# A transformer block in seven-product matmuls: first three column pairs interleaved at the start of mixer and FFN, one weight load moved, part of a norm moved to ScalarE

## The chip, the cores and the metric

One core of a Trainium2 chip runs the whole kernel. TensorE (PE) multiplies, VectorE (DVE), ScalarE (ACT) and GpSimd (POOL) work on tiles of 128 partitions, and SyncE (SP) issues most of the DMAs. The metric is device time in microseconds (us) of one execution; the median of three is 1564.4 us (1561.85 to 1564.85).

## The reference, cut to what matters

```
a = RMSNorm(x; norm_pre_mix)                       # x: 1024 tokens x 1024
q, k, v, r, low, u, sv, g1, g2 = split(a @ w_in)   # 1024 x 7184
y_gla = GLA(q, k, v, low; 4 heads, 64-token chunks) * silu(r) @ w_branch_gla
y_sgu = gelu(u) * spatial_mix(LayerNorm(gelu(sv))) @ w_branch_sgu
m  = sigmoid(g1) * y_gla + sigmoid(g2) * y_sgu
x1 = x  + RMSNorm(m @ w_out; norm_post_mix)
h  = RMSNorm(x1; norm_pre_ffn)
out = x1 + RMSNorm((silu(h @ w_a) * (h @ w_b)) @ w_ffn_out; norm_post_ffn)   # d_ff 2816
```

All of it is float32. GLA carries a state per head along 16 chunks of 64 tokens.

## The kernel before

**Products.** Each large matmul is done by the Strassen-Winograd scheme: seven half-size products instead of eight, with sums and differences of the quarters of both operands, and of the results. A product takes 12 matmuls of 128x512: four slices of the contraction, and for each slice three terms, because every operand is split into a high part (`hi`, a copy that ACT rounds to fp32r, L86) and a low part (`lo`, the rest, which DVE subtracts, L87). The three terms hi x hi, hi x lo, lo x hi are L110, L111 and L112 of `prod3`. So a product waits for an ACT instruction and then for a DVE instruction on both of its operands.

**Streams.** A `Pair` is two columns of 128 of a weight matrix: su, kq, v, r, sv, g1 and g2 are pairs of w_in (28 of them), f0 to f21 are pairs of w_ffn_in (22). `Pair.prepare(m)` makes product m's weight operand on DVE and ACT, `Pair.product(m)` runs its 12 matmuls, `collect` adds the result up. `Stream.todo` lists products in the order in which PE takes them; weights are prepared two ahead (`LEAD`). A lone pair goes 1, 7, 6, 5, 2, 4, 3. Only the first two pairs of a stream go in step, as 1, 2, 5, 7, 6, 4, 3 of both in turn, since at the start of a stream its left operand comes in piece by piece: products 1 and 2 need only tokens 512 to 1023 (`Operands.first`), product 5 needs the sum of two quarters of tokens 0 to 511 (`second`), product 4 one of them (`fourth`), and products 7, 6 and 3 need differences (`rest`).

**Stages.** x is loaded, normed, transposed on PE (tp_a) and split (the operand `a`; names ah5, al5 are hi and lo of product 5). The mixer stream runs 28 pairs; after its 14 first products the low-rank gate and then, as a background task stepped between products, the chunk states of GLA: u (update, PE), st (state, DVE, L599), o (readout, PE), on (ACT), ot (transpose). Two branch products follow, `bs` (ys) and `bl` (yg, seven products of 48 matmuls); yg's results are gated in `gla_final` by g1t and mt, loaded by SP into slots of the pool px (11 slots of 512 KB), and split into mh and ml. w_out multiplies mh, ml in four passes (token half and column half: 1,0; 1,1; 0,1; 0,0), each with eight weights w_wo, four of them in px. After the last two passes a token tile gets its two norms: `rs_pm` and `rs_pf` are inverse roots (a 128x1 power on POOL), xr is the residual (DVE, L1058), mix its normed copy (DVE, L1062). `Hs.tile` transposes it (tp_h on PE, copies hraw on ACT) and the FFN stream begins.

**Order.** The tile framework's scheduler puts the instructions of the recorded program on each engine's queue; on a queue they run in order. A `tc.manual_schedule` keeps the recorded order for the engines it names, `tc.issue_after` puts an instruction behind another.

## Time and profile before

| | |
|---|---|
| median of three runs | 1564.4 us |
| profiled execution | 1566.38 us, span 1564.5 us (1.9 us lie around the span) |
| mean granted TensorE clock | 0.992 of 2.4 GHz |
| PE busy | 1531.6 us, 98% of the span |
| DVE busy | 1134.8 us, 73% |
| ACT busy | 655.1 us, 42% |
| POOL busy | 178.7 us, 11% |

PE's busy time counts a matmul from issue to its end, and successive matmuls overlap, so 98% doesn't mean that only 2% could be saved: at half the clock PE is as busy as at full clock and does half as much.

### The profile page before, as it was taken

How to read it: one execution, taken by the hardware profiler on the slowest of the kernel's cores; microseconds unless marked ns; L12 is line 12 of the kernel's file. 1: busy time of each engine (PE TensorE's matmuls, PEld its weight loads, DVE VectorE, ACT ScalarE, POOL GpSimd, SP SyncE). 2: the span in 40 equal slices, each digit the busy share in tenths (PEclk: the TensorE clock that was granted, in tenths of full speed). 3: DMA queues.
4: the chain of work that ended last, by engine and by line, in shares of the span. 5: the costliest groups of instructions: out<-in, count | busy, mean ns of one | idle time of the engine just before them, and what ended most of it. 6: DMA issues, size and time to landing. Idle time of an engine off the chain costs nothing.

```text
span 1564.5 us, 19759 instructions
## 1 busy us (share of the span) xinstructions
PE 1531.6 (98%) x7061; PEld 1249.5 (80%) x7061; DVE 1134.8 (73%) x1854; ACT 655.1 (42%) x1074; POOL 178.7 (11%) x274
## 2 busy tenths in 40 slices
PE   7999999999999999999999989999999999999998
PEld 5778777687888888888877868888888888888886
DVE  7956676577978878657686689777777777565547
ACT  8475334244344343533443663333333333363442
POOL 2211111102211111000000120111111100000002
PEclk9999999999999999999999999999999999999999
DMA  4433344245654464588972633565555543775653
GB/s 163 126 95 96 120 151 166 76 148 167 238 195 155 145 212 141 177 317 305 332 239 81 204 120 101 187 204 176 197 184 185 176 133 101 284 273 173 226 161 128
DMA packets 181812, 276.06 MB, mean 176 GB/s; under 512 B 10777, under 2 KB 108593, under 8 KB 181714
## 3 DMA queue, kind: packets, MB, share of 16 engines
q1 hardware_dynamic: 157714, 190.35, 38.0%
q0 software_dynamic: 24000, 84.44, 14.7%
q8 instruction: 56, 0.92, 0.2%
q14 instruction: 42, 0.34, 0.1%
HBM read 188.47 MB, written 86.28 MB: 176 GB/s over the span
## 4 chain that ended last, share of the span: by engine, by line
PE 91%; DVE 6%; issue 1%; ACT 1%; DMA 1%; POOL 0%; DVEq 0%; SPq 0%; POOLq 0%; ACTq 0%
PE f_m L110 9%; PE f_m L111 9%; PE f_m L112 9%; PE fo L110 4%; PE fo L112 4%; PE fo L111 4%; PE g_m L110 3%; PE g_m L111 3%; PE g_m L112 3%; PE wo L112 2%; PE wo L111 2%; PE wo L110 2%; PE kq_m L112 2%; PE kq_m L111 2%; PE v_m L112 2%; PE v_m L111 2%
## 5 line engine op out<-in xcount | busy, mean ns | idle before, releaser
L110 PE MATMUL f_m<-hh,w_f 128*128 128x512 f32 x616 | 240.7, 391 | 5.2 <-ACT hh L86 5.2
L111 PE MATMUL f_m<-hl,w_f 128*128 128x512 f32 x616 | 240.4, 390 | 0.0
L112 PE MATMUL f_m<-hh,w_f 128*128 128x512 f32 x616 | 240.2, 391 | 0.0
L110 PEld LDWEIGHTS f_m<-hh,w_f 128*128 128x128 f32 x616 | 116.1, 189 | 29.9 <-ACT hh L86 5.8
L111 PEld LDWEIGHTS f_m<-hl,w_f 128*128 128x128 f32 x616 | 116.2, 189 | 24.2
L112 PEld LDWEIGHTS f_m<-hh,w_f 128*128 128x128 f32 x616 | 116.1, 188 | 24.2
L111 PE MATMUL fo<-fow,foa 128*128 128x512 f32 (+1 forms) x315 | 120.9, 384 | 0.0
L112 PE MATMUL fo<-fow,foa 128*128 128x512 f32 (+1 forms) x315 | 120.9, 384 | 0.0
L110 PE MATMUL fo<-fow,foa 128*128 128x512 f32 (+1 forms) x315 | 118.9, 385 | 0.5 <-DVE foc L914 0.5
L87 DVE TENSOR_TENSOR w_f<-wsum_f,w_f 128x512 fp32r<-128x512 f32 x88 | 60.5, 688 | 51.2 <-ACT w_f L86 50.7
L86 ACT ACTIVATE w_f<-wsum_f 128x512 fp32r<-128x512 f32 x88 | 55.3, 629 | 99.2 <-PE f_m L112 59.3
L111 PE MATMUL g_m<-al,w_g 128*128 128x512 f32 x224 | 88.3, 394 | 0.0
L110 PE MATMUL g_m<-ah,w_g 128*128 128x512 f32 x224 | 88.1, 393 | 0.0
L112 PE MATMUL g_m<-ah,w_g 128*128 128x512 f32 x224 | 87.8, 392 | 0.0
L86 ACT ACTIVATE w_f<-raw_f 128x512 fp32r<-128x512 f32 x66 | 41.4, 630 | 101.6 <-PE f_m L112 93.1
L87 DVE TENSOR_TENSOR foa<-fora,foa 128x1024 fp32r<-128x1024 f32 (+1 forms) x42 | 47.6, 1133 | 42.7 <-ACT foa L86 42.6
L86 ACT ACTIVATE foa<-fora 128x1024 fp32r<-128x1024 f32 (+1 forms) x42 | 41.5, 988 | 73.4 <-DMA fora<-fs_d 58.0
L110 PEld LDWEIGHTS fo<-fow,foa 128*128 128x128 f32 x315 | 59.2, 188 | 12.4 <-DVE foc L914 0.7
L111 PEld LDWEIGHTS fo<-fow,foa 128*128 128x128 f32 x315 | 59.2, 188 | 11.8
L112 PEld LDWEIGHTS fo<-fow,foa 128*128 128x128 f32 x315 | 59.2, 188 | 11.7
L87 DVE TENSOR_TENSOR fow<-forw,fow 128x1024 fp32r<-128x1024 f32 (+1 forms) x42 | 47.5, 1130 | 9.9 <-ACT fow L86 9.6
L112 PE MATMUL wo<-w_wo,ml 128*128 128x512 f32 x128 | 50.2, 396 | 2.6 <-DVE ml L87 2.6
(379 smaller groups left out, 3694.2 us busy)
## 6 DMA issues: line engine op xcount, KB each, us to landing
raw_f<-in_w_ffn_in SPq DMA_DIRECT2D x88, 256.0 KB, 3.3
fora<-fs_d SPq DMA_DIRECT2D x35, 512.0 KB, 4.5
w2e<-in_w_ffn_out SPq DMA_DIRECT2D x44, 256.0 KB, 4.3
fs_d<-f_o POOLq DMA_DIRECT2D x22, 512.0 KB, 3.8
ws_d<-w2e POOLq DMA_DIRECT2D x22, 512.0 KB, 3.8
forw<-ws_d SPq DMA_DIRECT2D x20, 512.0 KB, 4.6
raw_g<-in_w_in SPq DMA_DIRECT2D x16, 512.0 KB, 3.7
g_d<-g_o POOLq DMA_DIRECT2D x16, 512.0 KB, 4.2
```

Source lines behind the costliest of these rows:

```text
L86: a = nc.scalar.activation(hi, src, AF.Copy)
L87: return a, nc.vector.tensor_tensor(out=lo, in0=src, in1=hi, op=ALU.subtract)
L110: nc.tensor.matmul(acc, lhsT=lh, rhs=rh, start=first, stop=False, skip_group_check=onto)
L111: nc.tensor.matmul(acc, lhsT=lh, rhs=rl, start=False, stop=False, skip_group_check=onto)
L112: nc.tensor.matmul(acc, lhsT=ll, rhs=rh, start=False, stop=last, skip_group_check=onto)
```

## The change

It has five parts. (1) Both streams begin with three pairs: products 1 and 2 of the first two in turn, then 1 and 2 of the third, then 5, 7, 6, 4 and 3 of all three in turn. The third pair's raw weights live in the pool `pl`, its products take a buffer from both PSUM pools. For these pairs the weight differences are made in place, and product 5's result is copied straight into its half of the output tile. In the mixer the three pairs are fetched ahead, and the low-rank sums come after six products, where they came after four. (2) `fourth` is done just ahead of `rest`'s last part. (3) The weights of w_out's first pass are loaded and split between the two branches, where they were loaded during the second. (4) The second norm of token tiles 0, 1 and 2 is a scaled copy on ACT in place of DVE's three-operand instruction; its gain is applied when the transposed tile is copied, which takes eight 128x128 copies in place of two 128x512. Tile 3 stays as it was. (5) As the FFN begins, PE keeps the recorded order for its first 21 products, some weights are prepared behind named instructions, and the first silu (with its table load) is put behind the hi part of product 7's operand; until then the result is copied plainly.

```diff
-        def tile(self, row, tt):
+        def tile(self, row, tt, gains=None):
             r = 1 - tt // 4
             cols = slice((tt % 4) * P, (tt % 4) * P + P)
             for c in range(2):
                 b = tbank(f"tp_{self.name}{tt}{c}")
                 for j in range(4):
                     nc.tensor.transpose(b[:, j * P : (j + 1) * P], row[:, (c * 4 + j) * P : (c * 4 + j + 1) * P], ident)
-                nc.scalar.activation(self.quad(r, c)[:, :, cols], by4(b), AF.Copy)
+                if gains is None:
+                    nc.scalar.activation(self.quad(r, c)[:, :, cols], by4(b), AF.Copy)
+                    continue
+                for j in range(4):
+                    nc.scalar.activation(self.quad(r, c)[:, j, cols], b[:, j * P : (j + 1) * P], AF.Copy,
+                                         scale=gains[:, c * 4 + j : c * 4 + j + 1])
...
+                if m == 3:
+                    for i in range(2):
+                        nc.vector.tensor_tensor(out=s4[i], in0=a12[:, two[i]], in1=s1[:, two[i]], op=ALU.subtract)
+                    for tt in range(4):
+                        self.fourth(tt)
...
-                    self.last = split(hi[:, two[i]], lo[:, two[i]], src)[1]
+                    ins = split(hi[:, two[i]], lo[:, two[i]], src)
+                    self.last = ins[1]
+                    if m == 7:
+                        self.hi7 = ins[0]
...
+            self.trio = False
+            self.pool = (pr, "raw")
...
-                t = pr.tile([P, 4, 256], F32, tag="raw", name=f"raw_{self.name}{k}")
+                t = self.pool[0].tile([P, 4, 256], F32, tag=self.pool[1], name=f"raw_{self.name}{k}")
...
+                src = w12 if self.trio and m == 7 else py.tile([P, 4, P], F32, tag="Y", name=f"wsum_{self.name}{m}")
...
+            new = tbank if self.trio and m == 6 else bank
...
-                    self.p5 = [slot(f"{self.name}_p5", (P, 512))]
+                    self.out[1] = slot(f"{self.name}_o1")
+                    self.p5 = [self.out[1][:, 512:1024]]
...
+        def __init__(self, pairs, A):
             self.A = A
-            self.todo = []
-            self.hold = 11 if twin else 0
-            if twin:
-                a, b = pairs[:2]
-                self.todo += [(p, m) for m in (1, 2, 5, 7, 6, 4, 3) for p in (a, b)]
-                pairs = pairs[2:]
-            for p in pairs:
+            self.hold = 17
+            trio = pairs[:3]
+            for p in trio:
+                p.trio = True
+            trio[2].pool = (pl, "L")
+            self.todo = [(p, m) for part in (trio[:2], trio[2:]) for m in (1, 2) for p in part]
+            self.todo += [(p, m) for m in (5, 7, 6, 4, 3) for p in trio]
+            for p in pairs[3:]:
                 self.todo += [(p, m) for m in ORDER]
...
-                p.prepare(m)
+                with tc.issue_after(behind[self.ready].ins) if self.ready in behind else ExitStack():
+                    p.prepare(m)
...
-        wa = pl.tile([P, KT, 32], F32, tag="L", name="wa")
+        wa = slot("wa", (P, KT, 32))
...
     low_rank_weights()
-    stream.run(4)
+    stream.fetch(3)
+    stream.run(6)
     low_rank_sums()
-    for tt in (0, 1, 2, 3):
-        A.fourth(tt)
-    stream.run(2)
+    stream.run(3)
     A.rest()
-    stream.run(8)
+    stream.run(11)
     heads[0]["decays"] = bg.add(decays(*low_rank()))
-    stream.run(28, 2)
+    stream.run(22, 2)
...
-    bs.run()
-    bl.run()
...
+    wo = I["w_out"][0]
+
+    def out_weights(half, j):
+        return wide_weights(wo, list(range(KT)), j, f"wo{half}{j}", lambda k: (pw, "w") if k < 4 else (px, "X"))
+
+    bs.run()
+    wo10 = out_weights(1, 0)
+    bl.run()
...
+    first_silu = []
...
             if half == 1 and self.first:
-                with tc.issue_after(Hs.after[0].ins):
-                    nc.scalar.activation(o, src, func[0])
+                nc.scalar.activation(o, src, AF.Copy)
+
+                def silu():
+                    with tc.issue_after(Hs.hi7.ins):
+                        nc.scalar.activation(o, o, func[0])
+
+                first_silu.append(silu)
...
-        p.first = i % NK == 0
+        p.first = i % NK == 0 or i == 1
...
-        w = wide_weights(wo, list(range(KT)), j, f"wo{half}{j}", lambda k: (pw, "w") if k < 4 else (px, "X"))
+        w = wo10 if (half, j) == (1, 0) else out_weights(half, j)
...
-                xt = load(f"xr_{tt}", x[tt * P : (tt + 1) * P, :])
+                if tt in (2, 3):
+                    xt = slot(f"xr_{tt}")
+                    nc.sync.dma_start(out=xt, in_=x[tt * P : (tt + 1) * P, :])
+                else:
+                    xt = load(f"xr_{tt}", x[tt * P : (tt + 1) * P, :])
...
                 rs = rsqrt_mean(ss[:, 3:4], D, f"pf{tt}")
-                nc.vector.scalar_tensor_tensor(out=mix, in0=xt, scalar=rs, in1=g_pf, op0=ALU.mult, op1=ALU.mult)
-
-                def after(mix=mix, tt=tt):
-                    Hs.tile(mix, tt)
+                light = tt in (0, 1, 2)
+                if light:
+                    nc.scalar.activation(mix, xt, AF.Copy, scale=rs)
+                else:
+                    last = nc.vector.scalar_tensor_tensor(out=mix, in0=xt, scalar=rs, in1=g_pf, op0=ALU.mult,
+                                                          op1=ALU.mult)
+
+                def after(mix=mix, tt=tt, light=light):
+                    Hs.tile(mix, tt, g_pfT if light else None)
...
-    fstream.run(4)
-    fstream.prepare(6)
-    for tt in (0, 1, 2, 3):
-        Hs.fourth(tt)
-    Hs.rest()
-    fstream.run(8)
+    fstream.fetch(3)
+    fstream.prepare(4)
+    lo5 = Hs.after[1]
+    behind.update({4: last, 5: last, 6: last, 7: last, 8: lo5, 9: lo5, 10: lo5, 11: lo5})
+    with tc.manual_schedule(engines={mybir.EngineType.PE}):
+        fstream.run(9)
+        with tc.issue_after(lo5.ins):
+            Hs.rest()
+        behind.clear()
+        for f in first_silu:
+            f()
+        fstream.run(12)
```

Three places show how the queues move.

PE, in the middle of the mixer, before: the last two matmuls of v3's product 6 (v3 is the fourth v pair), the transposes wspT of the spatial weights, and GLA's readout o_23 with what follows it (u, st, o, on, ot as above; the digits are head and step).

```order
L112 MATMUL v3_m6_2670<-ah6_527,w_v36_2590 128x512
L581 MATMUL u_261_2645<-v_21_2358,kk_2_2289 128x256 x2
L691 MATMUL wspT_2660<-ident_106,wsp_2528 128x128 x4
L608 MATMUL o_23_2712<-st_233_2688,kq2_o1_1793 64x256
L608 MATMUL o_23_2712<-st_232_2687,kq2_o1_1793 64x256
L608 MATMUL o_23_2712<-st_231_2686,kq2_o1_1793 64x256
L608 MATMUL o_23_2712<-st_230_2685,kq2_o1_1793 64x256
L696 MATMUL rowsum_2717<-wT_2659,allone_2531 128x512
L635 MATMUL ot_230_2762<-ident_106,on_22_2650 128x128 x2
L635 MATMUL ot_231_2768<-ident_106,on_22_2650 128x128 x2
```

The same place in the change; ahead of these rows stand v3's product 6, readout o_20, updates u_22, wspT and the rest of o_21.

```order
L630 MATMUL o_21_2642<-st_210_2615,kq2_o1_1729 64x256
L603 MATMUL u_240_2647<-v_21_2482,kk_2_2418 128x256
L603 MATMUL u_241_2648<-v_21_2482,kk_2_2418 128x256
L603 MATMUL u_240_2647<-v_21_2482,kk_2_2418 128x256
L603 MATMUL u_241_2648<-v_21_2482,kk_2_2418 128x256
L718 MATMUL rowsum_2653<-wT_2589,allone_2458 128x512
L657 MATMUL ot_210_2698<-ident_106,on_20_2580 128x128 x4
L657 MATMUL ot_211_2704<-ident_106,on_20_2580 128x128 x4
L630 MATMUL o_22_2765<-st_223_2737,kq2_o1_1729 64x256
L630 MATMUL o_22_2765<-st_222_2736,kq2_o1_1729 64x256
```

Before, one state step stood between product 6 and product 5 of v3; now three (o_20, o_21, o_22) stand there, with no product between them.

DVE, as yg ends, before: ygc are the sums of yg's results, gated by g1t and mt, ml01 the lo part that w_out's first pass needs.

```order
L873 TENSOR_TENSOR ygc10_6687<-yg_72_6451,ygc01_6264 128x512
L87 TENSOR_TENSOR w_wo104_6827<-raw_wo104_6825,w_wo104_6827 128x512
L873 TENSOR_TENSOR ygc10_6687<-yg_73_6452,ygc01_6264 128x512
L957 TENSOR_TENSOR ygc10_6687<-ygc10_6687,g1t100_6691 128x512 x2
L957 TENSOR_TENSOR ygc10_6687<-ygc10_6687,g1t102_6711 128x512 x2
L958 TENSOR_TENSOR ygc10_6687<-ygc10_6687,mt100_6694 128x512 x2
L873 TENSOR_TENSOR ygc01_6264<-yg_50_6526,ygc01_6264 128x512
L958 TENSOR_TENSOR ygc10_6687<-ygc10_6687,mt102_6714 128x512
L87 TENSOR_TENSOR w_wo105_6830<-raw_wo104_6825,w_wo105_6830 128x512
L958 TENSOR_TENSOR ygc10_6687<-ygc10_6687,mt102_6714 128x512
L873 TENSOR_TENSOR ygc01_6264<-yg_51_6527,ygc01_6264 128x512
L87 TENSOR_TENSOR w_wo106_6835<-raw_wo106_6833,w_wo106_6835 128x512
```

The same place in the change.

```order
L894 TENSOR_TENSOR ygc10_6718<-yg_70_6480,ygc01_6295 128x512
L87 TENSOR_TENSOR ml11_6622<-ygc11_6543,mh11_6621 128x512
L894 TENSOR_TENSOR ygc10_6718<-yg_71_6481,ygc01_6295 128x512
L894 TENSOR_TENSOR ygc10_6718<-yg_72_6482,ygc01_6295 128x512
L894 TENSOR_TENSOR ygc10_6718<-yg_73_6483,ygc01_6295 128x512
L978 TENSOR_TENSOR ygc10_6718<-ygc10_6718,g1t100_6722 128x512 x2
L978 TENSOR_TENSOR ygc10_6718<-ygc10_6718,g1t102_6742 128x512 x2
L979 TENSOR_TENSOR ygc10_6718<-ygc10_6718,mt100_6725 128x512 x2
L979 TENSOR_TENSOR ygc10_6718<-ygc10_6718,mt102_6745 128x512 x2
L87 TENSOR_TENSOR ml01_6721<-ygc10_6718,mh01_6720 128x512
L894 TENSOR_TENSOR ygc01_6295<-yg_50_6557,ygc01_6295 128x512
```

The splits of w_wo are gone from this stretch (all eight of them stand between rows of ys now), and the ml01 splits follow the gating of ygc10 at once.

ACT, as the FFN begins, before: hh5, hh4 and hh7 are the hi parts of the left operand for products 5, 4 and 7, f0_o0 and f11_o0 the outputs to which the silu is applied.

```order
L86 ACTIVATE hh5_7522<-hraw20_7520 128x4x128
L86 ACTIVATE hh4_7732<-hraw11_7518 128x4x128
L86 ACTIVATE hh5_7522<-hraw20_7520 128x4x128
L1025 ACT_TABLE_LOAD
L1025 ACTIVATE f0_o0_7711<-f0_m1_7661 128x512
L1025 ACTIVATE f11_o0_7730<-f11_m1_7679 128x512
L86 ACTIVATE hh7_7744<-hraw10_7511 128x1024 x2
L86 ACTIVATE hh6_7752<-hraw20_7520 128x1024 x2
```

The same place in the change.

```order
L86 ACTIVATE w_f15_7794<-wsum_f15_7792 128x512
L1052 ACTIVATE f1_o0_7790<-f1_m1_7758 128x512
L86 ACTIVATE w_f07_7813<-raw_f00_7605 128x512
L86 ACTIVATE hh7_7852<-hraw10_7510 128x1024 x2
L1056 ACT_TABLE_LOAD
L1056 ACTIVATE f0_o0_7734<-f0_o0_7734 128x512
L1056 ACTIVATE f11_o0_7751<-f11_o0_7751 128x512
L1056 ACTIVATE f1_o0_7790<-f1_o0_7790 128x512
L318 ACTIVATE f0_o1_7810<-f0_m5_7797 128x512
L86 ACTIVATE w_f117_7832<-raw_f110_7614 128x512
```

The table load and the silus stood ahead of hh7; now they stand behind it, but w_f15, w_f07 and three plain copies of outputs (two of them some rows earlier) stand ahead.

## Rows read from the trace of the kernel before

**Rows 1.** The page, busy time, share of the span and instructions of each engine.

```profile
PE 1531.6 (98%) x7061; PEld 1249.5 (80%) x7061; DVE 1134.8 (73%) x1854; ACT 655.1 (42%) x1074; POOL 178.7 (11%) x274
```

**Rows 2.** PE's waits, whole span: what for; us in total, times, longest.

```profile
PE f_m L110 <- ACT hh L86: 5.2, 2, 2.6
```

**Rows 3.** Windows: length, busy us and instructions by engine, PE clock, DMA share, GB/s.

```profile
0.00:20.00 20.00, 9.97 (x36) 6.40 (x36) 13.04 (x24) 15.11 (x28) 7.42 (x20) 1.00 0.92 318
...
920.00:940.00 20.00, 13.68 (x63) 10.75 (x61) 19.54 (x29) 14.34 (x24) 4.62 (x4) 0.88 0.25 79
```

**Rows 4.** Window of the first 14 products, PE's su_m matmuls alone.

```profile
22.10:72.90 50.80, 42.53 (x168) 0.95 0.22 64
```

**Rows 5.** Groups of PE instructions in 22 to 73.2.

```profile
L452 PE MATMUL al<-araw,wa 128*32 128x256 f32 x64 | 3.7, 380 | 0.0
```

**Rows 6.** Timeline of PE, mid mixer: start, busy us, [idle before <-releaser].

```profile
309.26 1.08 PE L608 MATMUL o<-st,kq_o 128*64 128x256 f32 x8 [2.41 <-DVE st L599]
```

**Rows 7.** Timeline of PE where yg ends and w_out begins.

```profile
816.76 0.39 PE L110 MATMUL yg<-yga,ygw 128*128 128x512 f32 x1
...
818.57 0.39 PE L112 MATMUL yg<-yga,ygw 128*128 128x512 f32 x1
...
824.61 0.50 PE L112 MATMUL wo<-w_wo,ml 128*128 128x512 f32 x1 [2.56 <-DVE ml L87]
...
829.52 0.39 PE L111 MATMUL wo<-w_wo,mh 128*128 128x512 f32 x1
```

**Rows 8.** Timeline of PE as the FFN begins.

```profile
927.70 1.03 PE L170 MATMUL tp_h<-ident,mix 128*128 128x128 f32 x8
928.49 0.48 PE L112 MATMUL f_m<-hh,w_f 128*128 128x512 f32 x1
...
937.07 1.22 PE L110 MATMUL f_m<-hh,w_f 128*128 128x512 f32 x2 [2.65 <-ACT hh L86]
...
942.18 0.39 PE L112 MATMUL f_m<-hh,w_f 128*128 128x512 f32 x1
```

**Rows 9.** Timeline of ACT around the FFN's start.

```profile
912.14 0.19 ACT L1060 ACTIVATION_READ_ACCUMULATOR mix<-xr 128x1 f32 x1
912.24 1.66 ACT L86 ACTIVATE w_f<-raw_f 128x512 fp32r<-128x512 f32 x3
...
933.67 1.28 ACT L1025 ACT_TABLE_LOAD   x1
...
935.96 2.19 ACT L86 ACTIVATE hh<-hraw 128x1024 fp32r<-128x1024 f32 x2
```

**Rows 10.** ACT groups by shape: count, busy us, mean ns of one, idle before.

```profile
L623 ACT ACTIVATE on<-o 128x256 f32<-128x256 f32 x32 | 12.0, 380 | 11.5 <-PE o L608 11.0 <-PE u L581 0.6
...
L636 ACT ACTIVATE oT<-ot,vecs 128x512 f32<-128x512 f32 x16 | 10.6, 687 | 12.7 <-PE ot L635 12.7
...
L171 ACT ACTIVATE hraw<-tp_h 128x512 f32<-128x512 f32 x16 | 8.7, 593 | 8.8 <-PE tp_h L170 8.8
```

**Rows 11.** DVE groups by shape, the same columns.

```profile
L87 DVE TENSOR_TENSOR foa<-fora,foa 128x1024 fp32r<-128x1024 f32 x35 | 42.8, 1222 | 25.9 <-ACT foa L86 25.8
...
L599 DVE SCALAR_TENSOR_TENSOR st<-st,decay,u 128x256 f32<-128x256 f32 x60 | 28.6, 477 | 7.4 <-PE u L581 6.2
...
L87 DVE TENSOR_TENSOR w_wo<-raw_wo,w_wo 128x512 fp32r<-128x512 f32 x32 | 20.7, 683 | 7.5 <-ACT w_wo L86 7.5
```

**Rows 12.** Tile rs_pf: ns min/median/max, first and last start us.

```profile
L101 POOL TENSOR_TENSOR rs_pf<-rs_pf,mhalf x8: 558/564/2073, 860.8 to 926.6; 128x1 f32<-128x1 f32 x8
L1062 DVE SCALAR_TENSOR_TENSOR mix<-xr,rs_pf,gain_norm_pre_ffn x8: 1274/1282/1286, 861.4 to 928.7; 128x1024 f32<-128x1024 f32 x8
```

**Rows 13.** Tile g1t, 740 to 840: its use on DVE and its loads.

```profile
L957 DVE TENSOR_TENSOR ygc<-ygc,g1t x12: 677/679/683, 798.9 to 829.3; 128x512 f32<-128x512 f32 x12
...
L940 SPq DMA_DIRECT2D g1t<-g_d x3: 359/360/879, 753.6 to 780.2; - x3
...
DMA to landing us min/median/max: 5.7/7.7/9.7
```

22 lines of the change are left out of this document (10 added, 12 removed).

## The prediction

> **What bounds the kernel now.** First the page: PE is busy 98% of the span, DVE 73%, ACT 42% [rows 1]. An average says little here, so I went on to the list of PE's waits. Its largest entry is 5.2 us in two waits of the FFN's products for ACT's hi parts [rows 2]. So what a change can win lies in a few places, and I looked at each in the timeline, counting matmuls. In steady state the starts of nine matmuls from 816.76 to 818.57 lie 0.227 us apart [rows 7]; a product of twelve takes 2.72. What a stretch lasts beyond matmuls times 0.227 is its loss. Four places stand out.
>
> *Mixer start.* The first 14 products, 168 matmuls, take the 50.8 us from 22.1 to 72.9, at a mean clock of 0.95 of 2.4 GHz [rows 4]. 168 x 0.227 = 38.1; the low-rank matmuls in between take 3.7 [rows 5]; three groups of eight transposes at 0.79 (927.70 to 928.49 shows one such group, [rows 8]) make 2.4. Loss: 50.8 - 44.2 = 6.6 us.
>
> *Mid mixer.* PE is idle for 2.41 us until the state st of a GLA step is ready on DVE [rows 6].
>
> *w_out's start.* From yg's last matmul at 818.57 to 829.52 PE does 23 matmuls (yg's last, eight before and 14 after the idle time shown): 10.95 - 5.2 = 5.7 us lost. The largest part is 2.56 us in which it waits for the lo part ml [rows 7]; DVE has w_wo splits among the sums there (the order's rows above), each 0.68 [rows 11].
>
> *FFN start.* From 928.49 to 942.18 PE does 15 matmuls and one group of transposes: 13.7 - 3.4 - 0.8 = 9.5 us lost [rows 8]. ACT loads a table at 933.67 and applies silus until 935.96; only then comes the hi part of product 7, for which PE waits 2.65 us [rows 8, 9]. DVE is busy 19.54 of the 20 us from 920 [rows 3], so it is the engine that would bind next.
>
> The clock adds to each: in 920 to 940 its mean is 0.88 [rows 3], and the two matmuls at 937.07, behind the wait, take 1.22 us, where 0.227 + 0.39 is the normal length of two [rows 8]: they run at 1.2 GHz. What such matmuls cost is in the losses above already.
>
> **The change part by part.**
>
> *Mixer start, -3.3 us.* Six products now stand ahead of the first product 5, where four stood, and three of a kind give DVE and ACT 8.2 us for each step's operands where two gave 5.4. Walking DVE's queue with 0.60 a 128x512 and 1.14 a 128x1024 (0.68 and 1.22 [rows 11], less the 0.08 by which neighbours overlap), every weight and operand from product 5 on is ready 5 us or more before PE's turn. What stays is the cold start and the first pieces' latency, about 2. Against it, half of the third pair's first weight block (256 KB) is now loaded ahead of x: at the 318 GB/s of the first 20 us [rows 3] 0.8 us, and up to 1.5 if its neighbour is slowed too. 6.6 - 2 - 1.3 = 3.3. Bounds: 1 (half of the stalls come back) and 5 (no delay of x).
>
> *Mid mixer, +1.5 us.* Nothing here is meant to change, but the background steps fall elsewhere: three GLA steps stand together with no product between them (the order's rows above). Each step costs PE a wait until DVE has made four updates at 0.48 [rows 11] after the last update product. The first costs about what it costs now, 2.41 [rows 6]; the second is partly, the third mostly covered by rowsum and eight transposes. Bounds 0 (all covered) and +3 (one more whole wait of 2.41 with matmuls at half clock behind it); 1.5 lies between.
>
> *w_out's start, -4.7 us.* All eight w_wo splits (8 x 0.60 = 4.8 us of DVE) leave the stretch. The first part of ml is ready when PE's wait ends, at 824.6 [rows 7]. In the change three w_wo splits and three ygc01 sums no longer stand among ygc10's rows ahead of it (6 x 0.60 = 3.6), and further up four splits are gone, of which I count 2.1 us, since DVE would wait for PE in the rest: 818.9. PE needs it at 819.25. The later parts come every 1.2 us where PE takes one every 0.68, so about 1 us stays lost: 5.7 - 1.0 = 4.7; bounds 3 and 5.7. The moved work isn't free by itself: 4 DMAs of 512 KB, 8 ACT and 8 DVE instructions at ys's end. It is hidden by DVE's idle time there (it waits for PE's ys products), and five early g1t and mt loads of 512 KB give way to the four. Without that cover it costs DVE's 4.8 us.
>
> *FFN start, -7.5 us.* ACT's part first. Tile 1's sum of squares ends at 912.3 (912.14 + 0.19), and the three copies of 0.63 behind it take 1.66, so neighbours overlap by 0.1 [rows 9]. In the change there stand behind it, up to the end of tile 3's sum of squares: seven 128x512 at 0.5, two scaled copies of 1024 columns at 1.0 (two such take 2.19 at most, [rows 9]), two sums of squares at 1.2, one of 512 columns at 0.7 (0.19 is the read of the sum), and 16 scaled copies of 128x128. That last form isn't in the trace. From 512 to 256 columns a copy falls from 0.593 to 0.380, so 128 columns would take 0.27, and a scale read from a tile adds 0.09 (0.687 against 0.593) [rows 10]; less an overlap of 0.1 that is 0.27 a copy. Bounds: 0.18 (no price of the scale) and 0.38 (a whole copy of 256 columns). With 0.27: 912.3 + 3.5 + 2.0 + 2.4 + 0.7 + 4.3 = 925.2. POOL's power takes 0.56 as a median [rows 12], with handoffs 0.8: tile 3's norm starts on DVE at 926.0 and ends at 927.3. PE wants its transposes at 929.0, so the wait for them, 1.2 now, goes.
>
> Then DVE. From 926.0 to the lo part of f1's product-7 weight its queue holds the norm (1.28, [rows 12]), 20 of 128x512 at 0.60 and ten of 128x1024 at 1.14: 926.0 + 1.2 + 12.0 + 11.4 = 950.6. PE ends w_out at 916.1 (928.49 less 47 matmuls and two groups of transposes), does 11 products (29.9) and three transposed tiles (2.4), and needs that lo part two matmuls on: 948.9. So PE waits 1.7 us there or in instalments ahead of it, and 0.3 for two later weights. Product 7's hi part is ready some 4 us early, since the table load stands behind it. 9.5 - 2.0 = 7.5. With 0.18 and 0.38 a copy the queue shifts by -1.4 and +1.8, and POOL's longest power, 2.07 [rows 12], would add 1.2: bounds 9.2 and 4.5.
>
> The Trainium skill speaks against this part twice. "ScalarE: Activation LUTs", section "What ACT_TABLE_LOAD costs", gives a copy with a scale pointer 280 ns + 0.833 a column, less 93 of overlap: 0.294 us for 128 columns by its figures; rows of this trace agree at 512 columns (0.687 against 0.706 by the page). With it the sum would be 0.4 us smaller. Its "Rules for kernel authors" put a multiplication on VectorE. Here 1024 columns of float32 take ACT 1.1 and DVE 1.28 [rows 9, 12], so the rows decide for ACT.
>
> *Nothing:* product 5 straight into the output tile, in-place differences, the second PSUM pool and one more small vector save slots and add no instruction that PE waits for; ahead of them lie two or more products (5.4 us). Were a slot late, one landing of a load would show.
>
> *Sum:* -3.3 + 1.5 - 4.7 - 7.5 = -14.0. The profiled execution took 1566.4, so 1552.4; it stood 2.0 above the median of 1564.4, so the median comes to **1550.4 us**. From the bounds: -1 + 3 - 3 - 4.5 = -5.5 and -5 + 0 - 5.7 - 9.2 = -19.9, that is 1558.9 and 1544.5.
>
> **The rivals.**
>
> *ACT becomes the bound of the FFN's start.* The change takes 3.6 us from DVE and gives ACT three scaled copies (2.9) and 24 small ones for 6. If these cost 0.38 or more each and POOL is slow, tile 3's norm comes 3 us later, and DVE's whole queue with it: loss 5 to 6 instead of 2. For it: ACT is on the path to every power. Against: DVE, not ACT, was at 19.54 of 20 us [rows 3]. The sum is -10: 1554.5. The Trainium skill's rule on multiplications (the same page and section) points this way.
>
> *The reshuffled order loses more elsewhere.* x late by 1.5, the cluster in mid mixer at +3, and the mixer's start wins 1: -1 + 3 - 4.7 - 7.5 = -10.2; with one more such cluster that I overlooked, -7: 1554 to 1557.
>
> *The stalls only move.* DVE's work is the same, and it is the next bound in three of the four places. If each wait comes back further down as a wait for DVE's backlog, what is left is below 3 us: 1561.5 to 1567.5. Against: DVE is idle for over a quarter of the span [rows 1], and the change puts more products ahead of each need, not fewer.
>
> *Slower: the slots.* w_out's four early weights hold four of px's 11 slots through all of yg, so the eight pairs of g1t and mt loads start later. Before, the last g1t load was issued at 780.2, 49 us ahead of its last use at 829.3; landing took 7.7 us as a median [rows 13]. Now it can start only when an earlier gate's slot is free. Were landings exposed on DVE, which holds everything behind it in its queue, each would cost up to 7.7; from the third on it eats more than the 14 us, and four make 31 - 14 = +17: 1581; three 1573. Against: in the order a load still stands some ten DVE instructions and more ahead of its use; I see 3 us of slack or more at each.
>
> **How the numbers follow.** My forecast has 0.60, with a range of its own of 1546 to 1555; ACT as the bound 0.15, order losses 0.12, stalls that only move 0.07, slots 0.06. From 1544.5 to 1558.9 the first three lie almost whole; 1544 to 1559 leaves out the last two and a little, under 2 in 10. 0.2% is 3.1 us, about what a measurement of this kernel can tell: faster 0.87, same 0.07, slower 0.06.
>
> **What would show it.** Right: FFN products no longer in PE's list of waits for hh; tp_h without a wait; a wait of 1 to 2 us for a lo weight around 945; w_wo's first rows at ys's end; no wait above 1 us between yg and wo; a mean clock of 0.98 and more in the windows of w_out's and the FFN's start; in mid mixer two or three waits for st close together. ACT's 128x128 copies at a pitch of 0.2 to 0.38. Wrong: DVE's sums at yg's end waiting for g1t or mt; tp_h or product 5 waiting for ACT's small copies; the first products of su more than 2 us later than 22.1.

## The result, and the profile after

Four runs of the changed kernel have a median of 1552.82 us (1551.24 to 1553.29); four of the kernel before, on the same chip, 1563.87 (1561.85 to 1564.85). The ratio is 0.9929, with a 95% interval of 0.9912 to 0.9946: faster by 11.0 us. The profiled execution took 1552.86 us where that of before took 1566.38, 13.5 less. The forecast was 14.0 less on the profiled execution, and 1550.4 for the median.

The page's first part of the changed kernel answers to [rows 1]:

```profile
PE 1523.6 (98%) x7061; PEld 1243.9 (80%) x7061; DVE 1130.2 (73%) x1853; ACT 661.6 (43%) x1100; POOL 177.8 (11%) x275
```

PE's share is the same 98% although 13.6 us of the span are gone: the share says nothing of such stalls. DVE has 4.6 us less work, ACT 6.5 more. PE's waits (answering to [rows 2]; us in total, times, longest) say more. The three largest, not shown, lie ahead of the first product, all but 0.99 us of them:

```profile
PE o L630 <- DVE st L621: 3.2, 1, 3.2
PE f_m L110 <- ACT w_f L86: 1.1, 1, 1.1
...
PE ot L657 <- DVE st L621: 0.8, 1, 0.8
PE f_m L110 <- ACT f_u L302: 0.7, 1, 0.7
```

The 5.2 us for hh are gone, and so is the wait for ml; in mid mixer the wait for st has grown. Where PE does idle, the timeline shows (start, busy us, [idle before <-releaser]); the rows at 926.50 and 955.24 answer to [rows 8], those at 301.66 and 307.87 to [rows 6], and for [rows 7] there is no idle row left to show:

```profile
23.29 1.20 PE L110 MATMUL su_m<-ah,w_su 128*128 128x512 f32 x2
25.48 1.94 PE L170 MATMUL tp_a<-ident,a 128*128 128x128 f32 x8 [0.99 <-DVE a L406]
...
301.66 1.84 PE L630 MATMUL o<-st,kq_o 128*64 128x256 f32 x8 [3.15 <-DVE st L621]
...
307.87 0.66 PE L657 MATMUL ot<-ident,on 128*128 128x128 f32 x4 [0.77 <-DVE st L621]
...
926.50 0.50 PE L110 MATMUL f_m<-hh,w_f 128*128 128x512 f32 x1 [0.69 <-ACT f_u L302]
...
955.24 0.47 PE L110 MATMUL f_m<-hh,w_f 128*128 128x512 f32 x1 [1.13 <-ACT w_f L86]
```

The windows (length; busy us and instructions of PE, PEld, DVE, ACT, POOL; PE clock; DMA share, GB/s) answer to [rows 3]. Half clock (1.2 of 2.4 GHz: matmuls of 512 columns then start 0.43 us apart, at 27.64 and 28.07 for instance, and not 0.227) is left in the first products and in mid mixer, and gone where w_out and the FFN begin.

```profile
20.00:40.00 20.00, 17.20 (x79) 14.43 (x80) 15.73 (x24) 16.23 (x31) 4.02 (x6) 0.83 0.19 49
...
300.00:320.00 20.00, 17.57 (x80) 12.14 (x81) 13.53 (x31) 6.53 (x14) 1.43 (x2) 0.91 0.19 56
820.00:840.00 20.00, 20.00 (x90) 16.55 (x89) 12.24 (x20) 6.88 (x15) 0.00 (x0) 1.00 0.06 18
...
920.00:940.00 20.00, 19.31 (x89) 15.76 (x88) 19.90 (x27) 16.88 (x30) 0.00 (x0) 1.00 0.00 1
```

**Where the 13.6 us of span come from.** Two tiles serve as landmarks. The view of a tile lists a line's matmuls with their shortest, median and longest ns and the start of the first and the last; L112 is the third term of a product. First the kernel before, then a second profile of it taken with the experiments, then the changed kernel:

```profile
L112 PE MATMUL yg<-yga,ygw x112: 388/389/389, 743.1 to 818.6; 128*128 128x512 f32 x112
...
L112 PE MATMUL f_m<-hh,w_f x616: 389/389/632, 916.6 to 1351.1; 128*128 128x512 f32 x154
```

```profile
L112 PE MATMUL yg<-yga,ygw x112: 388/389/389, 742.3 to 817.8; 128*128 128x512 f32 x112
...
L112 PE MATMUL f_m<-hh,w_f x616: 389/389/632, 913.4 to 1347.4; 128*128 128x512 f32 x154
```

```profile
L112 PE MATMUL yg<-yga,ygw x112: 389/389/390, 742.1 to 817.6; 128*128 128x512 f32 x112
...
L112 PE MATMUL f_m<-hh,w_f x616: 387/389/474, 909.8 to 1337.5; 128*128 128x512 f32 x154
```

Up to yg's last row lies the mixer, from there to f_m's first the start of w_out, from f_m's first to its last the FFN with its start; from then to the end of the span it is 213.4 us in all three. I divide the mixer at the 168th matmul of its products, counted in the timeline: it starts at 72.79 in the kernel before, 72.14 in its second profile, 71.43 after.

| stretch | forecast | after less first profile | after less second |
|---|---|---|---|
| mixer start, to the 168th matmul | -3.3 | -1.4 | -0.7 |
| rest of the mixer | +1.5 | +0.4 | +0.5 |
| w_out's start (98.0, 95.6, 92.2 us) | -4.7 | -5.8 | -3.4 |
| FFN (434.5, 434.0, 427.7 us) | -7.5 | -6.8 | -6.3 |
| sum | -14.0 | -13.6 | -9.9 |

The profiles of the experiments below tell how far single executions can be trusted. w_out's start took 92.2 or 92.3 us in all eleven profiles with its first weights moved, and the FFN 427.7 us in all six with the FFN of the changed kernel (the changed kernel, experiments 1, 2, 3, 9 and 10), so differences of half a microsecond count there. The mixer's doesn't repeat so well: in the six profiles with the changed kernel's mixer (the changed kernel, experiments 3 and 5 to 8) the 168th matmul starts between 70.60 and 72.74, the rest of the mixer takes 745.3 to 746.2 us, and yg ends between 815.9 and 818.0. The rest of the mixer took 745.8 and 745.7 us in the two profiles of the kernel before, so its +0.4 can't be told from nothing.

### The profile page after: what moved, and what is told of

Read it like the earlier page. It is cut to its first block, busy times and chain, and to the rows that moved or that the text cites. A ratio compares the mean times of both kernels' runs of the same rounds, so it can differ in the third digit from the quotient of the medians.

```text
span 1550.9 us, 19786 instructions
## 1 busy us (share of the span) xinstructions
PE 1523.6 (98%) x7061; PEld 1243.9 (80%) x7061; DVE 1130.2 (73%) x1853; ACT 661.6 (43%) x1100; POOL 177.8 (11%) x275
## 4 chain that ended last, share of the span: by engine, by line
PE 94%; DVE 3%; ACT 1%; issue 1%; DMA 0%; POOL 0%; SPq 0%; DVEq 0%; POOLq 0%; ACTq 0%
PE f_m L110 8%; PE f_m L112 8%; PE f_m L111 8%; PE fo L110 5%; PE fo L111 5%; PE fo L112 5%; PE g_m L110 3%; PE g_m L112 3%; PE g_m L111 3%; PE wo L110 2%; PE wo L111 2%; PE wo L112 2%; PE kq_m L110 2%; PE su_m L111 2%; PE kq_m L112 2%; PE su_m L112 2%
## 5 line engine op out<-in xcount | busy, mean ns | idle before, releaser
L112 PE MATMUL f_m<-hh,w_f 128*128 128x512 f32 x616 | 239.5, 389 | 0.0
L112 PEld LDWEIGHTS f_m<-hh,w_f 128*128 128x128 f32 x616 | 115.6, 188 | 24.2 <-DVE w_f L87 0.2
L112 PE MATMUL fo<-fow,foa 128*128 128x512 f32 (+1 forms) x315 | 120.9, 384 | 0.0
L86 ACT ACTIVATE w_f<-raw_f 128x512 fp32r<-128x512 f32 x75 | 47.2, 633 | 104.7 <-PE f_m L112 88.5
L86 ACT ACTIVATE w_f<-wsum_f 128x512 fp32r<-128x512 f32 x79 | 49.9, 633 | 95.2 <-PE f_m L112 52.8
L87 DVE TENSOR_TENSOR w_f<-wsum_f,w_f 128x512 fp32r<-128x512 f32 x79 | 54.3, 688 | 48.1 <-ACT w_f L86 47.6
L112 PE MATMUL g_m<-ah,w_g 128*128 128x512 f32 x224 | 87.8, 392 | 0.0
L112 PEld LDWEIGHTS fo<-fow,foa 128*128 128x128 f32 x315 | 59.2, 188 | 11.8
L87 DVE TENSOR_TENSOR w_f<-raw_f,w_f 128x512 fp32r<-128x512 f32 x75 | 51.2, 685 | 4.1 <-ACT w_f L86 3.9
```

The source lines that it names most:

```text
L86: a = nc.scalar.activation(hi, src, AF.Copy)
L87: return a, nc.vector.tensor_tensor(out=lo, in0=src, in1=hi, op=ALU.subtract)
L112: nc.tensor.matmul(acc, lhsT=ll, rhs=rh, start=False, stop=last, skip_group_check=onto)
```

## The experiments

Below, "w_out's start" is the time between the two landmarks, "FFN" that of f_m from first to last. Each run is compared with the kernel before on the same chip; the changed kernel stands at 0.9929.

**1. Third pair's weights loaded behind x.** The changed kernel loads 256 KB of kq's weights ahead of x on SP's queue; here they come after x's last piece.

```diff
                 if tt == 1:
                     stream.fetch(2)
+                if tt == 3:
+                    stream.fetch(3)
...
-    stream.fetch(3)
     stream.run(6)
```

> The changed kernel, with the third pair's raw weights (kq) fetched behind all of x, in the recorded order of SP's queue. My theory: in the changed kernel the mixer's start won only 1 us because 256 KB of kq went ahead of x (first sum of squares at 6.38 us, 4.85 before) and because tile 1's transposes stand behind only two matmuls, so that PE idles 0.99 us and runs at half the clock until 28.5. Both should go: first square near 4.85, first product near 22.2, no half clock after 25, and a span 2 to 4 us shorter than 1550.9, about 1548. Rival (the order in the first 20 us does not matter, since DVE's queue behind it is the limit from product 5 on): the same span within 1 us, with the time that is won showing up as waits for w_su or w_kq between 45 and 70 us.

Measured: 1550.97 us (1550.24 to 1551.0), ratio 0.9913 (0.9900 to 0.9927). yg ends at 815.8, 1.8 earlier than in the changed kernel, and all of it is there by the 168th matmul (69.69 against 71.43). In the changed kernel ACT's first square starts at 6.38 behind an idle 4.30 us for x; before it was 4.85, here it is 4.92. The first product starts as late as in the changed kernel, so it isn't x's delay that makes it late. But what follows it isn't torn apart:

```profile
21.66 1.94 PE L170 MATMUL tp_a<-ident,a 128*128 128x128 f32 x8 [6.14 <-DVE a L406]
23.25 1.20 PE L110 MATMUL su_m<-ah,w_su 128*128 128x512 f32 x2
...
30.41 1.91 PE L170 MATMUL tp_a<-ident,a 128*128 128x128 f32 x16
```

Here two groups of transposes come without idle time at 30.41. In the changed kernel one stood behind only two matmuls, at 25.48, and waited 0.99 us, and half clock went on until 28.5. So x's delay of 1.5 us cost 1.8. It isn't the scatter of single executions: the six profiles with x late have the 168th matmul at 70.60 to 72.74, the five with x first (experiments 1 and 9 to 12) at 68.98 to 70.06, in the mean 1.9 earlier. How much of it is half clock varies: in experiments 3 and 6, with x late, only the first two matmuls are slow, and the 168th still starts at 70.84 and 70.60. Three things that I expected were missed: a span 2 to 4 us shorter (1.8), a first product near 22.2 (23.25), and no half clock after 25 (it lasts until 26.4).

**2. Two pairs in the mixer, as before; the FFN with three.**

```diff
...
-    stream = Stream([pair(k, i) for k, i in plan], A)
+    stream = Stream([pair(k, i) for k, i in plan], A, True)
...
-    stream.fetch(3)
-    stream.run(6)
+    stream.run(4)
     low_rank_sums()
-    stream.run(3)
-    A.rest()
-    stream.run(11)
+    for tt in (0, 1, 2, 3):
+        A.fourth(tt)
+    stream.run(2)
+    A.rest(False)
+    stream.run(8)
...
-    stream.run(22, 2)
+    stream.run(28, 2)
```

> The changed kernel, with the mixer's stream begun as before: two pairs in turn, low-rank sums after four products, no early fetch of kq. All else is changed. My theory: the mixer as a whole gained only 1.0 us (yg's last matmul at 817.6 against 818.6), so the span is 1552 (+1), with the waits of before in it: 0.95, 1.39 and 0.40 us before 62 us and 2.4 us for the state in mid mixer. Rival (what was forecast, three pairs worth 3.3 at the start): 1554 or more. Second rival (three pairs cost as much as they win): 1550 to 1551.

Measured: 1555.28 us (1555.23 to 1557.22), ratio 0.9946 (0.9932 to 0.9959); yg ends at 819.9, 2.3 later than with three. The waits that three pairs removed are back, with one of 1.43 at the next pair:

```profile
59.41 0.47 PE L110 MATMUL su_m<-ah,w_su 128*128 128x512 f32 x1 [1.19 <-ACT w_su L86]
...
62.11 0.80 PE L110 MATMUL su_m<-ah,w_su 128*128 128x512 f32 x1 [1.00 <-DVE su_u L308]
...
92.03 0.50 PE L110 MATMUL kq_m<-ah,w_kq 128*128 128x512 f32 x1 [1.43 <-DVE kq_u L308]
...
310.43 1.35 PE L632 MATMUL o<-st,kq_o 128*64 128x256 f32 x8 [2.41 <-DVE st L623]
```

In mid mixer it is the single wait of 2.41 us again, as in [rows 6]. So the three pairs are worth 2.3 us here net of x's delay and of the longer mid-mixer wait; the span, 1553.2, lies between the theory and its rival. Not all of it need be the third pair: the 168th matmul starts at 73.89 here, 1.1 and 1.8 later than in the two profiles of the kernel before, which has two pairs as well, and why I couldn't place.

**3. w_out's first weights loaded where they were before.**

```diff
-    wo10 = out_weights(1, 0)
...
-        w = wo10 if (half, j) == (1, 0) else out_weights(half, j)
+        w = out_weights(half, j)
```

> The changed kernel, with the weights of w_out's first pass loaded and split during yg's end again, as before. My theory: DVE's splits among yg's last sums were the whole of the loss there, so the span is 5 to 6 us longer, 1556 to 1557, and PE waits for mh and ml again (1.0 and 2.6 us) with matmuls at half the clock behind it. Rival (the early three-pair start or other shifts moved DVE's backlog too): less than 3 us longer.

Measured: 1556.07 us (1554.46 to 1557.61), ratio 0.9947 (0.9933 to 0.9960); w_out's start 96.2 against 92.2. Its wait and its clock:

```profile
820.37 0.50 PE L112 MATMUL wo<-w_wo,ml 128*128 128x512 f32 x1 [2.09 <-DVE ml L87]
```

```profile
820.00:840.00 20.00, 19.63 (x79) 16.11 (x80) 13.73 (x23) 6.32 (x14) 0.00 (x0) 0.91 0.18 59
```

Moving the load is worth 4.0 us: 2.09 of idle, the rest is the half clock behind it. The wait for mh that I expected didn't come back, and the span is only 2.5 us longer, not 5 to 6: 1.5 is hidden, because in this execution yg ended at 816.1, 1.5 earlier than in the changed kernel's. Nothing was changed ahead of it; that is the mixer's scatter.

**4. The kernel before, once more**, unchanged, for a second profile.

> The kernel before, unchanged, profiled once more. Its first profiled execution took 1566.4 us, 2.5 above the median of its runs, and in it one power on GpSimd took 2.07 us where the median is 0.56, just ahead of the last norm of the FFN's start. Theory: that was chance, the power takes 0.56 to 0.94 this time, the transposes tp_h do not wait 1.2 us, and the span is 1562 to 1563. Rival (a profiled execution of this kernel is always some 2 us longer): a span near 1564.5 with a power of 2 us again or another wait of that size.

Measured: 1562.7 us, span 1560.8, which is 3.7 less than the first profile's. The theory named the wrong place for it: a power of 2.07 us on GpSimd came again, and so did the wait of 1.16 us for tp_h. The wait for ml is the same as in [rows 7]:

```profile
823.10 0.50 PE L112 MATMUL wo<-w_wo,ml 128*128 128x512 f32 x1 [2.55 <-DVE ml L87]
```

But the granted clock of 820 to 840 was 0.91 in the first profile and is 1.00 here:

```profile
820.00:840.00 20.00, 17.44 (x69) 13.94 (x70) 16.69 (x28) 7.21 (x14) 0.00 (x0) 0.91 0.26 80
```

```profile
820.00:840.00 20.00, 17.45 (x77) 14.12 (x76) 15.77 (x27) 5.94 (x13) 0.00 (x0) 1.00 0.25 80
```

In the first execution PE also waited 0.99 us for mh, here 0.22. So 2.4 us of w_out's loss in the first profile came and went from one execution to the next, 0.8 of it this wait and 1.6 half clock. In the FFN's start the clock is 0.83 and 1.00 (920 to 940, 940 to 960) where it was 0.88 and 0.95, about the same in sum.

**5. The second norm back on DVE.** DVE's three-operand instruction for all tiles, transposed tiles copied two at a time.

```diff
-                light = tt in (0, 1, 2)
+                light = tt in ()
```

> The changed kernel, with the second norm of all four last token tiles on DVE as before (three 128x1024 three-operand instructions and six 128x512 copies in place of three scaled copies and 24 small ones on ACT). Measure: the FFN stream's third terms, first to last start, 427.7 us in the changed kernel (909.8 to 1337.5), 434.5 in the kernel before. My theory: DVE was idle some 4 us before tile 3's norm at 918.3 anyhow, and ACT gets 6 us lighter, so the move is worth under 1 us: 427.7 to 428.7. Rival (DVE's queue is the bound all the way, so its 3.6 us come back): 431 or more.

Measured: 1552.20 us (1551.2 to 1553.65), ratio 0.9922 (0.9906 to 0.9939). FFN 428.2 against 427.7. The norm on ACT brings half a microsecond, which the median doesn't show; the theory, under 1 us, holds.

**6. PE's order free as the FFN begins.**

```diff
-    with tc.manual_schedule(engines={mybir.EngineType.PE}):
+    with ExitStack():
```

> The changed kernel, without the fixed TensorE order as the FFN begins; the scheduler then puts f0's and f11's product 5 into f1's product 2, single matmuls of product 7 ahead of f1's product 5, and ends products in other places. My theory: a matmul that comes early waits for an operand that is still in DVE's queue and holds all behind it, so the FFN stream takes 1 to 2 us more than 427.7. Rival (three pairs are enough, the order adds nothing): within 0.5 us. Other rival (the order is the main part of the 6.8 us): 431 or more.

Measured: 1551.78 us (1550.77 to 1553.16), ratio 0.9922 (0.9908 to 0.9937), FFN 427.6. The fixed order is worth nothing, as the first rival had it.

**7. The first silus where they were**, behind product 5's operand, with the table load ahead of product 7's hi part.

```diff
-                nc.scalar.activation(o, src, AF.Copy)
-
-                def silu():
-                    with tc.issue_after(Hs.hi7.ins):
-                        nc.scalar.activation(o, o, func[0])
-
-                first_silu.append(silu)
+                with tc.issue_after(Hs.after[0].ins):
+                    nc.scalar.activation(o, src, func[0])
```

> The changed kernel, with the first silus applied straight from PSUM and put behind product 5's operand as before, so that the table load and silus stand ahead of product 7's hi part again. My theory: in the changed kernel that hi part is ready at 932.6, 4 to 5 us ahead of PE's turn, so up to 3 us on ACT are covered by three products 5 and the FFN stream stays within 1 us of 427.7. Rival (the table load and the silus were the cause of PE's 2.65 us wait, as the timeline of before reads, and still are): 429.5 to 430.5, with a wait for hh.

Measured: 1555.56 us (1553.56 to 1555.96), ratio 0.9943 (0.9929 to 0.9958), FFN 431.2: 3.5 us longer. That is beyond the theory and its rival, and the wait isn't the rival's, for product 7's hi part. ACT's queue, then PE's only wait in 918 to 935:

```profile
925.34 1.28 ACT L1053 ACT_TABLE_LOAD   x1
926.64 1.08 ACT L1053 ACTIVATE f_o<-f_m 128x512 f32<-128x512 f32 x2
927.61 0.60 ACT L302 ACTIVATE f_u<-f_m 128x512 f32<-128x512 f32 x1
```

```profile
928.26 0.80 PE L110 MATMUL f_m<-hh,w_f 128*128 128x512 f32 x1 [2.83 <-ACT f_u L302]
```

f1's product 2 is accumulated in the bank of its product 1, which ACT has to copy out to f_u first. That copy stands behind the table load and two silus. In the changed kernel the same matmul is the one at 926.50, with 0.69 us.

**8. Two pairs in the FFN; the mixer with three.** The norm on ACT, the late silus and the fixed order stay.

```diff
...
-        p.first = i % NK == 0 or i == 1
+        p.first = i % NK == 0
...
-    fstream = Stream([gated(i) for k in range(NK) for i in (k, NK + k)], Hs)
+    fstream = Stream([gated(i) for k in range(NK) for i in (k, NK + k)], Hs, True)
...
-    behind.update({4: last, 5: last, 6: last, 7: last, 8: lo5, 9: lo5, 10: lo5, 11: lo5})
+    behind.update({4: last, 5: last, 6: lo5, 7: lo5})
...
-        fstream.run(9)
+        fstream.run(6)
...
```

> The changed kernel, with only two pairs in turn as the FFN begins; the mixer keeps its three, and the norm on ACT, the fixed TensorE order and the late silus stay. My theory: the third pair's products are what covers the queues of ACT and DVE, so most of the gain goes: FFN stream 431 to 434. Rival (the lighter DVE queue, the order and the late silus are what wins): 428 to 429.5.

Measured in ten runs: 1563.34 us (1561.52 to 1563.9), ratio 0.9991 (0.9982 to 1.0000). FFN 438.2: 10.5 us longer than with three pairs, and 3.7 longer than before the change. PE's larger waits:

```profile
925.10 0.50 PE L110 MATMUL f_m<-hh,w_f 128*128 128x512 f32 x1 [2.18 <-ACT hh L86]
...
941.40 0.50 PE L112 MATMUL f_m<-hh,w_f 128*128 128x512 f32 x1 [1.48 <-DVE w_f L87]
...
950.38 0.47 PE L110 MATMUL f_m<-hh,w_f 128*128 128x512 f32 x1 [3.41 <-DVE f_u L308]
```

So without the third pair's products the FFN's gain is gone, and more: the other edits of its start win nothing by themselves. That the third pair is the cover fits this, but a third pair alone, without the other edits, was not run, and how much of the 10.5 is due to the order, which was laid out for three pairs, was not tried.

Runs 9 to 12 start from the kernel of experiment 1, and look for what is left.

**9. The chunk states let loose earlier,** after 14 products as before the change, not 20.

```diff
-    stream.run(11)
+    stream.run(5)
...
-    stream.run(22, 2)
+    stream.run(28, 2)
```

> e1_x_first, with the background task of the mixer (the GLA chunks' steps) let loose after 14 products as in the kernel before, not after 20. Theory: the pair of waits around 300 us (3.15 us for st and 0.77 us for the next st, with the half clock behind it) comes from where the cluster of the last chunk's small products meets the weight sum of the fourth pair, which stays at one place in the order; so nothing is gained: w_out's start within 0.7 us of e1_x_first's 815.8 us, time 1550 to 1552 us. Rival: spreading the steps earlier loosens the cluster, 2 to 4 us shorter (1547 to 1549 us).

Measured: 1556.57 us (1555.21 to 1557.85), ratio 0.9958 (0.9942 to 0.9975), yg's end at 820.2: 4.4 later. Neither account had that. The wait in mid mixer stays (2.87 us for st), and a new one comes at 107.68, where ACT has the gate's table load ahead of the copy PE waits for:

```profile
107.68 0.50 PE L110 MATMUL v_m<-ah,w_v 128*128 128x512 f32 x1 [2.18 <-ACT v_u L302]
```

```profile
105.25 1.28 ACT L551 ACT_TABLE_LOAD   x1
...
107.03 0.59 ACT L302 ACTIVATE v_u<-v_m 128x512 f32<-128x512 f32 x1
```

PE's idle rows from 60 to 330 us add up to 7.0 against 5.0 in experiment 1; half clock is about equal in sum. That is 2.0 of the 4.4; the other 2.4 I couldn't place.

**10. The all-ones tile in a slot of its own.** The row sums of the spatial weights are a product with an all-ones tile, which held one of the two buffers of tag `Y` that product 5's weight sum also takes.

```diff
-        allone = py.tile([P, P], F32, tag="Y", name="allone")
+        allone = slot("ones_all", (P, P))
```

> e1_x_first, with the all-ones tile of the row sums in a slot of its own pool instead of one of the two buffers that the weight sums of the fifth product also take. Theory: the 3.15 us wait for st near 301 us comes from the fifth product's weight sum of the fourth pair, which waits for that buffer until the row sum has been multiplied, so that the small products of the last chunk stand next to each other on TensorE with nothing between; with the buffer free, products of the pair stand between them, the idle times of 3.15 and 0.77 us go and the clock stays high there (0.91 in 300:320 now): w_out starts at 811 to 813.5 us instead of 815.8, time 1546 to 1549 us. Rival: the waits come from DVE's own chain and only move to the next product: within 1 us of e1_x_first (1550 to 1552 us).

Measured: 1545.84 us (1544.92 to 1546.43), ratio 0.9886 (0.9872 to 0.9901). yg ends at 810.2, 5.6 earlier than in experiment 1 and beyond the range expected. In mid mixer PE shows no idle time, products stand between the small matmuls, and the clock of 300 to 320 is 1.00:

```profile
294.80 1.08 PE L630 MATMUL o<-st,kq_o 128*64 128x256 f32 x8
...
296.88 0.66 PE L713 MATMUL wspT<-ident,wsp 128*128 128x128 f32 x4
297.29 0.48 PE L111 MATMUL v_m<-al,w_v 128*128 128x512 f32 x1
```

```profile
300.00:320.00 20.00, 20.00 (x98) 14.21 (x97) 15.05 (x34) 6.83 (x18) 2.15 (x3) 1.00 0.20 66
```

In the changed kernel wspT is followed by the wait of 3.15 us, and the weight sum of product 5 comes at 308.24, behind the row sums at 305.38:

```profile
305.38 1.13 PE L718 MATMUL rowsum<-wT,allone 128*128 128x512 f32 x2
...
308.24 0.68 DVE L257 TENSOR_TENSOR wsum_v<-raw_v 128x512 f32<-128x512 f32 x1
```

One buffer made the cluster. Of experiment 1's idle time 4.1 us (3.15, 0.77 and one of 0.16) are gone, and the half clock. Another 0.7 of the 5.6 was there by the 168th matmul already (68.98 against 69.69), where nothing was changed: that is scatter. What the buffer is worth is 4.9: the rest of the mixer takes 741.2 us here and in experiment 12, 746.1 and 745.9 in experiments 1 and 11.

**11. The FFN's first six products in another order,** so that f1's product 2 doesn't follow its product 1 at once.

```diff
-            self.todo = [(p, m) for part in (trio[:2], trio[2:]) for m in (1, 2) for p in part]
+            self.todo = [(trio[i], m) for i, m in ((0, 1), (1, 1), (0, 2), (2, 1), (1, 2), (2, 2))]
```

> e1_x_first, with the FFN's first six products in the order pair 0 product 1, pair 1 product 1, pair 0 product 2, pair 2 product 1, pair 1 product 2, pair 2 product 2, so that pair 1's second product, which accumulates onto the bank that ACT copies out after the first, does not follow the first at once. Theory: the 0.69 us wait for f_u near 925 us goes, and f_m from first to last takes 426.8 to 427.3 us instead of 427.7; time 0.4 to 0.9 us shorter than e1_x_first (1550.0 to 1550.6 us). Rival: another pair's product 2 waits for ACT instead, 0 to 2 us longer.

Measured: 1551.46 us (1550.74 to 1551.75), ratio 0.9922 (0.9907 to 0.9937), FFN 428.3: 0.6 longer. The wait for f_u is gone, and a longer one for a weight's lo part is there instead, as is the one for w_f:

```profile
942.23 0.51 PE L112 MATMUL f_m<-hh,w_f 128*128 128x512 f32 x1 [1.28 <-DVE w_f L87]
...
954.22 0.47 PE L110 MATMUL f_m<-hh,w_f 128*128 128x512 f32 x1 [1.15 <-ACT w_f L86]
```

PE reaches DVE's backlog that much sooner: a stall that did only move.

**12. Both,** the edits of 10 and 11 together.

> e11_allone and e12_spread together. If both theories hold, the gains add: 1545.5 to 1548.5 us, w_out's start at 811 to 813.5 us and f_m's stretch 426.8 to 427.3 us. If neither does, 1550 to 1552 us, as e1_x_first.

Measured: 1546.51 us (1546.18 to 1546.96), ratio 0.9891 (0.9877 to 0.9906), yg's end at 810.9, FFN 428.4. The first edit pays, the second costs 0.6 again. The best kernel is that of run 10, at 1545.84: 17.1 us below the kernel before (1562.89 on that chip).

## Why the prediction was right, and where it was off

The direction, the places and the sum on the profiled execution held (-13.5 us for -14.0). The median came 2.4 us above the forecast. That the sum came so close is in part luck: against the first profile the mixer's start fell 1.9 short of its term and the FFN 0.7, while the rest of the mixer and w_out's start did better than theirs by 1.1 each. Against the second profile the sum is -9.9, and between the medians -11.0.

**The step that failed is the last one, from the profiled execution to the median.** The working took off 2.0 us, since the profiled execution of before stood that far above its median. But the losses of the sum were read from that same execution, and part of them was why it stood so high: w_out's start lost 2.4 us more there than in the second profile, 1.6 by half clock behind the wait for ml and 0.8 by a longer wait for mh. The change removed them there, so they could not be subtracted once more. The changed kernel's profiled execution lies 0.04 us from its median.

**Mixer start: right in kind, half the size.** -3.3 forecast, -1.4 and -0.7 measured; the lower bound was 1. The term was 4.6 of stalls won less 1.3 for x's delay. x came 1.5 us late, as its bound said, and that cost 1.8, or 1.9 in the mean of the profiles: what I left out is what the delay does to the order behind it, where a group of transposes waits after two matmuls. Experiment 1 undoes that, and then the step has -3.1 against the first profile and -2.5 against the second, where 4.6 were to be won. Most of what is missing is a term that the sum had at nothing: three pairs make the first product start 1.1 us later (23.15 to 23.31 in the five profiles with x first, 22.01 to 22.19 in the three with two pairs in the mixer). In DVE's queue of experiment 1 four weight sums and differences (L257) of 0.6 us each stand ahead of the norm that the last transposes before the first product wait for, where two stood in the kernel before, and that norm starts at 20.23, not 19.13. That they are the cause is read from the queue; no run tried it. The stalls from product 5 on are gone as forecast. "The first products more than 2 us later", a sign that it would be wrong, didn't come.

**Mid mixer: +1.5 forecast; the waits there grew by just that** (3.15 + 0.77 against 2.41 [rows 6]), and a wait of 0.96 for the gate at 107 us came on top, but the rest of the mixer as a whole is no longer than before. Where some 2 us came back I couldn't place, so the waits were forecast rightly and the length of the stretch was not. The second wait was 0.16 to 0.77 us in the six profiles with this mixer. The cause named, three state steps with no product between them, was right; why they stood together I had not asked. Experiment 10 shows it: one buffer.

**w_out's start: -4.7 forecast, -5.8 and -3.4 measured; experiment 3 gives 4.0** for the moved load by itself. No wait is left: DVE has the first ml part ready at 816.3, 1.2 us ahead of yg's last matmul, where I had it 0.3 behind. So the microsecond that was to stay lost went too.

```profile
815.67 0.68 DVE L87 TENSOR_TENSOR ml<-ygc,mh 128x512 fp32r<-128x512 f32 x1
```

**FFN start: -7.5 forecast, -6.8 and -6.3 measured.** The waits for hh and for the transposes are gone. ACT's small copies, whose price was the open bound, were nearly as estimated; ACT's timeline of the changed kernel:

```profile
907.44 0.61 ACT L86 ACTIVATE w_f<-raw_f 128x512 fp32r<-128x512 f32 x1
907.96 2.15 ACT L175 ACTIVATE hraw<-tp_h,vecs 128x128 f32<-128x128 f32 x8
909.95 1.11 ACT L1096 ACTIVATE mix<-xr 128x1024 f32<-128x1024 f32 x1
```

ACT's timeline shows eight in 1.99 us, from 907.96 to the next start at 909.95, 0.25 each, where 0.27 was forecast. By the figures of the Trainium skill's page "ScalarE: Activation LUTs", section "What ACT_TABLE_LOAD costs", an estimate is 0.294; the trace is below it. On DVE tile 3's norm starts 9.0 us after PE passes from w_out to the FFN at 909.34 (9.9 forecast), and the lo part of f1's product-7 weight is ready 33.9 after it (34.5):

```profile
918.31 1.28 DVE L1102 SCALAR_TENSOR_TENSOR mix<-xr,rs_pf,gain_norm_pre_ffn 128x1024 f32<-128x1024 f32 x1 [0.74 <-POOL rs_pf L101]
...
942.52 0.68 DVE L87 TENSOR_TENSOR w_f<-raw_f,w_f 128x512 fp32r<-128x512 f32 x1
```

So DVE's queue was walked rightly, but PE doesn't wait at its end: the lo part is ready at 943.20 and the matmul that reads it starts at 943.40, since PE had lost time further up. What is left is 0.69 us for the copy of f1's product 1 on ACT and 1.13 for a weight's hi part on ACT, 1.8 in all where 2.0 was forecast for DVE: the size right, the first place wrong. I had looked at operands and weights of each product, not at the bank that it accumulates in. The second wait ends on ACT, but it is DVE's backlog after all, for ACT itself stood idle until DVE had made the difference:

```profile
954.60 1.15 ACT L86 ACTIVATE w_f<-raw_f 128x512 fp32r<-128x512 f32 x2 [1.17 <-DVE raw_f L265]
```

The wait for a lo part does come once the first of the two is taken away (experiment 11).

**The edits costed at nothing, and the attribution.** No wait for a slot, g1t, mt or product 5's output shows up, so the slower rival fell. ACT did not become the bound of the FFN's start, though both waits left there end on ACT, the second by way of DVE. That the stalls only move was wrong of the change and right of experiment 11. I had priced the FFN's start as a queue of edits to DVE's and ACT's work; the runs show that without the third pair it is gone (10.5 us in experiment 8), and that the late silus are worth 3.5, the norm on ACT 0.5 and the fixed order nothing. These don't add up to 6.8, since each is taken with the others in place; what the third pair wins alone was not run.

## What to carry to other kernels

A sum made from one execution's losses belongs to that execution: convert it to a median only after asking which of the losses are the reason that it stands off the median. When independent work is short at the start of a stream, a third strand to interleave can matter more than any one rearrangement of what each engine does, as in this FFN. And where small dependent steps pile up on an engine, look for the buffer that keeps the work between them from being prepared: here one 64 KB tile in the wrong pool cost 5 us.
